# Attention rows turned by VectorE through DRAM instead of by TensorE: one change to a hybrid conformer and mLSTM kernel

## The chip, the cores and the metric

The kernel runs on one core of one Trainium2 chip. The metric is the device time of one execution in microseconds. A core has TensorE (PE, matmuls; PEld is its weight loads), VectorE (DVE), ScalarE (ACT), GpSimd (POOL) and SyncE (SP), each with an instruction queue of its own that is worked off in order. DMAs are issued here from SP's queue (nearly all loads) and from ACT's queue (stores to scratch in DRAM).

## The reference

Two post-norm layers run over 256 latent tokens and 256 context tokens of width 1024. Layer 0 mixes tokens with a Conformer convolution module, layer 1 with a bidirectional chunkwise mLSTM of 4 heads of width 512. Each mixer is followed by a squared-ReLU MLP, and all is modulated by adaLN vectors. The output is the latent stream. The part that matters here is the mLSTM's output, for each head:

```python
hsum = of[..., :MLSTM_INNER] * from_heads(h_f) + of[..., MLSTM_INNER:] * from_heads(h_b)
hh = hsum.reshape(bsz, s, MLSTM_HEADS, MLSTM_HEAD_DIM)
mu = jnp.mean(hh, axis=-1, keepdims=True)
var = jnp.mean(jnp.square(hh - mu), axis=-1, keepdims=True)
hn = ((hh - mu) * lax.rsqrt(var + LN_EPS)).reshape(bsz, s, MLSTM_INNER) * gn_g
y = (hn + skip * xc) * jax.nn.silu(z)
return y @ w_down
```

`h_f` and `h_b` are attention-like sums over chunks, weighted by `exp` of cumulated forget gates; `of` is a sigmoid gate computed from the latent tokens by a 2048 to 4096 product.

## The kernel before

All activations lie in SBUF; weights are streamed from DRAM in pieces of 128x2048 (1 MB) into one of three `raw` buffers. Every product is done in three matmuls of fp32r (`mm3`, `mm3t`): a value is split into a high part, cast by ACT (L151, tile `wh` for weights), and a low part, subtracted by DVE (L152, `wl`). Weight halves of 128x1024 have four buffers each (`NW = 4`).

The mLSTM of layer 1 first computes features and scores. Turned copies go to DRAM: `v_dr` (values, turned by DVE in 32x32 blocks at L1261 and stored by ACT's queue at L1265), `zs_dr` (the silu of z and skip * xc, feature by token), `r_dr` (the residual rows).

Then comes the stage of the change. It is a set of Python generators, zipped by a hand-written table:

```python
att = [['o0', 'G0 W0 T0 W1', 2], ['o1', 'A0 W2', 1.6], ['o2', 'A1 W3 D0', 2.1], ['o3', 'A2 V3', 2], ['D1 E3 D2', 'A3', 3], ['D3', '', 0]]
```

Each entry has a main chain, a side chain and how many side steps are taken per main step. `o` is `gate_o(h)`, 16 steps of twelve 128x512 matmuls (two directions d, four weight pieces q of two halves, psums `mm`, of which there are three; the bias row `bo` is loaded at L1491). `G` is `decay` (the forget gates' cumulated sums, ending in a store to `ng_dr`), `W` is `weights(h)` (the exponentials, DVE and ACT only, from rows of `ng_dr` loaded at L1510), `T` is `guards`, `V` is `values`, `A` is `attend(h)`, `D` is `down(h)`, `E` is `early`. The table gives the order in which work is written; a scheduler then orders each engine's queue by that priority and by when it expects operands, and puts in the waits.

`attend(h)` has 11 steps: the values are loaded and split; four groups of matmuls into psums `cv` are scaled and gated (L1624) and summed per token block into `hs[0]` and `hs[1]` (128 tokens x 512 features); statistics; the load of `zs_dr` into a `raw` buffer; ACT normalises `hs` (L1642). Then for each half `jp` TensorE turns four times two 128x128 blocks into PSUM (L1650, psums `ln`), DVE multiplies by `gn_g` and adds skip * xc (L1654), multiplies by silu(z) (L1656) and the result is split for `down(h)`. Tiles of this stage are in pool `og` (13 buffers): `y` is written over `og[h, 1, jp]`.

`decay` has five steps; the matmuls of the sums are at L1435 and L1436, after two bare steps. The residual rows `R` (1 MB) are loaded at L1573 in the second half of `gate_o(0)`; `down(0)` is their first reader. The 408 columns of vectors (`vecs`, biases, gains, convolution weights) come in two loads: the first 64 columns first of all (L117), the other 344 after the second step of the first product (L657).

At the start, `start0(f)` loads a 1 MB piece of adaLN weights (L145), a block of x (L623) and of the first product's weights (L625) for each of eight f; L344 multiplies the adaLN piece.

Of the kernel before, what the change touches and what calls it, by code (L numbers as in the profile page):

```python
# [8 lines left out]
F32 = mybir.dt.float32  # L9
# [3 lines left out]
ALU = mybir.AluOpType  # L13

P = 128
# [6 lines left out]
C = 256  # L22
H = 4
DH = E // H
# [32 lines left out]
_OFF = {}  # L57
# [14 lines left out]
def hybrid_kernel(ctx: ExitStack, tc: tile.TileContext, xT, vecs_d, wdw_d, ada0_w, ada_w, wg_d, pw1a, pw1, pw2, w1_0, w2_0,  # L72
                  w1_1, w2_1, up_x, up_z, wv, wo, bo_d, wk, wq, wqT, wdown, rows_d, out):
    nc = tc.nc
# [6 lines left out]
    dp = ctx.enter_context(tc.tile_pool(name="dp", bufs=1, space=bass.MemoryType.DRAM))  # L81
# [3 lines left out]
    def nm(s):  # L85
        uid[0] += 1
        return f"{s}_{uid[0]}"
# [13 lines left out]
    def psum(tag="mm"):  # L101
        return pp.tile([P, 512], F32, tag=tag, name=nm(tag), bufs={"mm": 3, "ln": 2, "fl": 1, "cv": 2}[tag])
# [10 lines left out]


    vecs = con.tile([P, NV], F32, name="vecs")
    NV0 = _OFF["ada_b1"][0]
    nc.sync.dma_start(vecs[:, :NV0], vecs_d[:, :NV0])  # L117

    def V(name, i=0, n=1):
        o = _OFF[name][0]  # L120
        return vecs[:, o + i:o + i + n]
# [5 lines left out]
    ident = con.tile([P, P], F32, name="ident")  # L127
# [484 lines left out]
    x, u = [], []  # L612
# [7 lines left out]
    def start0(f):  # L620
        t = X()
        raw = raw_load(ada0_w[f])
        nc.sync.dma_start(t, xT[f * P:(f + 1) * P, :])  # L623
        wr = F()
        nc.sync.dma_start(wr[:, :KO0 * P], pw1a[f])  # L625
        x.append(t)
        ps = psum("fl")[:, :2 * P]
        ada_mm(ps, [raw[:, kt * 2 * P:(kt + 1) * 2 * P] for kt in range(DT)])
        sb = F()[:, :2 * P]
        with tc.issue_after(folded):  # L630
            st[f] = wr, sb, nc.vector.tensor_copy(sb, ps).ins
# [22 lines left out]
    start1(0)  # L654
    idle(spare, 5)
    start0(1)
    nc.sync.dma_start(vecs[:, NV0:], vecs_d[:, NV0:])  # L657
    for f in range(DT):
        start2(f, (0,))
        if f + 1 < DT:  # L660
# [17 lines left out]
    fj, jj = ij[:, 0:L], ij[:, L:2 * L]  # L678
# [517 lines left out]
    for f in range(0, DT, 2):  # L1196
        t, tr = tmp("S"), psum("cv")
# [194 lines left out]
    def decay(_):  # L1392
        gT = tmp("L")
        nc.scalar.copy(gT, gps)
        yield
        gk = psum("ln")
        for b in range(4):
            nc.tensor.matmul(gk[:, b * 16:(b + 1) * 16], gT[:, b * P:(b + 1) * P], foldg, start=True, stop=True)
        gs = tmp("S")[:, 0:64].rearrange("p (b c) -> p b c", b=4)
        nc.vector.tensor_tensor(gs, gk[:, 0:64].rearrange("p (b c) -> p b c", b=4),  # L1400
                                VA("b_gate").rearrange("p (b c) -> p b c", b=4), op=ALU.add)
        gb_ = [tmp("L"), tmp("E"), tmp("E")]
        g8 = [gb_[i // 3][:, (i % 3) * 4 * NG:(i % 3 + 1) * 4 * NG].rearrange("p (b c) -> p b c", b=4) for i in range(8)]
        ig, fg, bsb, ex, up1, cor, lf, fa = g8
        nc.vector.memset(ig, 0.0)
        nc.vector.memset(fg, 0.0)
        for d in range(2):
            nc.vector.tensor_copy(ig[:, :, 32 * d:32 * d + 4], gs[:, :, 8 * d:8 * d + 4])
            nc.vector.tensor_copy(fg[:, :, 32 * d:32 * d + 4], gs[:, :, 8 * d + 4:8 * d + 8])


        nc.vector.scalar_tensor_tensor(fa, fg, -1.0, fg, op0=ALU.mult, op1=ALU.max)
        nc.scalar.activation(ex, fa, AF.Exp, scale=-1.0)
        nc.vector.tensor_scalar(up1, ex, 1.0, None, op0=ALU.add)
        nc.vector.scalar_tensor_tensor(cor, up1, -1.0, ex, op0=ALU.add, op1=ALU.subtract)
        nc.scalar.activation(lf, up1, AF.Ln)
        nc.vector.reciprocal(up1, up1)
        nc.vector.tensor_tensor(cor, cor, up1, op=ALU.mult)
        nc.vector.tensor_tensor(lf, cor, lf, op=ALU.subtract)
        nc.vector.tensor_scalar(fa, fg, 0.0, None, op0=ALU.min)  # L1420
        nc.vector.tensor_tensor(lf, lf, fa, op=ALU.add)

        nc.vector.memset(up1, 0.0)
        for d, (b0, b1, b2, b3) in ((0, (0, 1, 2, 3)), (1, (1, 0, 3, 2))):
            c = slice(32 * d, 32 if d == 0 else NG)
            nc.vector.tensor_copy(up1[:, b1, c], lf[:, b0, c])
            nc.vector.tensor_tensor(up1[:, b2, c], up1[:, b1, c], lf[:, b1, c], op=ALU.add)
            nc.vector.tensor_tensor(up1[:, b3, c], up1[:, b2, c], lf[:, b2, c], op=ALU.add)
        yield
        yield  # L1430
        bps = psum("ln")
        for d, cum in ((0, upper), (1, lower)):
            c = slice(32 * d, 32 if d == 0 else NG)
            reg = bps[:, 0:4 * NG].rearrange("p (b c) -> p b c", b=4)[:, :, c]
            nc.tensor.matmul(reg, cum, lf[:, :, c], start=True, stop=False)  # L1435
            nc.tensor.matmul(reg, ones, up1[:, :, c], start=False, stop=True)  # L1436
        nc.vector.tensor_copy(bsb, bps[:, 0:4 * NG].rearrange("p (b c) -> p b c", b=4))
        nc.vector.tensor_tensor(acol, ig, bsb, op=ALU.subtract)

        yield  # L1440
        aT = psum("ln")
        for b in range(4):
            nc.tensor.transpose(aT[:NG, b * P:(b + 1) * P], acol[:, b, :], ident)
        aR, mR = tmp("S"), tmp("S")
        nc.vector.tensor_copy(aR[:32, :], aT[:32, :])
        nc.vector.tensor_copy(aR[32:NG, LO], aT[32:NG, LO])
        nc.vector.tensor_copy(aR[32:NG, HI], aT[32:NG, T - 1:C - 1:-1])
        nc.vector.tensor_tensor_scan(mR[:NG, :], aR[:NG, :], aR[:NG, :], 0.0, op0=ALU.max, op1=ALU.max)
        nc.vector.tensor_scalar(negm[:32, :], mR[:32, HI], -1.0, None, op0=ALU.mult)
        nc.vector.tensor_scalar(negm[32:NG, :], mR[32:NG, T - 1:C - 1:-1], -1.0, None, op0=ALU.mult)  # L1450
        nc.scalar.dma_start(ng_dr, negm)
        bsbs.append(bsb)
        yield
# [104 lines left out]
    for i in range(2):  # L1558
        rx = raw_load(xl_dr[i].rearrange("p b c -> p (b c)"))
        for j in range(8):  # L1560
            t = XL(F32R)
            split(t[:, LO], t[:, HI], rx[:, j * C:(j + 1) * C])
            xls.append((t[:, LO], t[:, HI]))
    og, yy, rden, sums = {}, {}, {}, {}

    def gate_o(h):

        for d in range(2):
            bo = rows(BO().rearrange("p a b -> p (a b)"), bo_d[h:h + 1, d * DH:(d + 1) * DH])
            pss = [psum() for _ in range(2)]  # L1570
            if (h, d) == (0, 1):
                with tc.issue_after(loaded[0]):
                    nc.sync.dma_start(R, r_dr)  # L1573
            for q in range(4):
                ws = preo if (h, d, q) == (0, 0, 0) else None
                if ws is None:
                    raw = raw_load(wo[h, d, q])
                for i in range(2):
                    w = ws[i] if ws else split_w(raw[:, i * 1024:(i + 1) * 1024])
                    for t in range(2):  # L1580
                        for k in range(2):
                            kt = 4 * q + 2 * i + k
                            sl = slice(k * 512, (k + 1) * 512)
                            mm3t(pss[t], xls[kt][0][:, BLK[t]], xls[kt][1][:, BLK[t]], w[0][:, sl], w[1][:, sl],
                                 kt == 0, kt == ET - 1)
                        if q == 3 and i == 1:
                            og[h, d, t] = o_ = OG()
                            nc.vector.tensor_tensor(o_, pss[t], bo, op=ALU.add)  # L1588
                            nc.scalar.activation(o_, o_, AF.Sigmoid)
                    yield  # L1590

    vsp, zt = {}, []

    def values(h):
        rv = raw_load(v_dr[h].rearrange("p b c -> p (b c)"))
# [7 lines left out]
    def attend(h):  # L1603
# [7 lines left out]
        hs = []  # L1611
        for t in range(2):
            for d in range(2):
                ps = psum("cv")
                bl = [b for b in blocks[d] if rng[d, b][0] <= t * P < rng[d, b][1]]
                for i, b in enumerate(bl):
                    hi, lo = pw[h, d, b]
                    sl = slice(t * P - rng[d, b][0], t * P - rng[d, b][0] + P)
# [13 lines left out]
        if h == H - 1:  # L1632
            zz = zt
        else:
            rz = raw_load(zs_dr[h].rearrange("p b c -> p (b c)"))
            zz = [rz[:, i * T:(i + 1) * T] for i in range(4)]
# [5 lines left out]
            nc.scalar.activation(hs[t], hs[t], AF.Identity, scale=mv[:, t, 2:3], bias=mv[:, t, 3:4])  # L1642
        yield
        yy[h] = []
        for jp in range(2):
            tr = psum("ln")
            for jj in range(2):
                j = 2 * jp + jj
                for t in range(2):
                    nc.tensor.transpose(tr[:, jj * C + t * P:jj * C + (t + 1) * P], hs[t][:, j * P:(j + 1) * P], ident)  # L1650
            y = og[h, 1, jp]
            for jj in range(2):
                j, sl = 2 * jp + jj, slice(jj * C, (jj + 1) * C)
                nc.vector.scalar_tensor_tensor(y[:, sl], tr[:, sl], V("gn_g", 4 * h + j), zz[2 + jp][:, sl],  # L1654
                                               op0=ALU.mult, op1=ALU.add)
            nc.vector.tensor_tensor(y, y, zz[jp], op=ALU.mult)  # L1656
            hi, lo = OG(F32R), OG(F32R)
            split(hi, lo, y)
            yy[h] += [(hi[:, sl], lo[:, sl]) for sl in (LO, HI)]
            yield  # L1660
# [373 lines left out]
```

## Time and profile before

| | us |
|---|---|
| median of 3 runs | 1664.04 (1663.55 to 1665.42) |
| the profiled execution's own time | 1665.14 |
| its span, first to last instruction | 1663.4 |
| TensorE matmul busy | 1648.7 (99%) |
| VectorE busy | 1038.1 (62%) |
| ScalarE busy | 734.6 (44%) |
| granted TensorE clock | 0.999 |

A line of the profile names a source line, an engine, an operation, the tiles it writes and reads, a count, then busy time and mean duration. "a <- b" in the list of waits means that a sat idle until b was done: total, times, longest. The chain of waits is the sequence of work that ended last; a piece in it lasts until the next begins, so it gives the pace of pipelined matmuls where their own duration does not. Rows marked SPq or ACTq are a queue issuing DMAs, which is not counted as busy time. Times in windows are from the start of the span.

### The profile page before, as it was taken

How to read it: one execution, taken by the hardware profiler on the slowest of the kernel's cores; microseconds unless marked ns; L12 is line 12 of the kernel's file. 1: busy time of each engine (PE TensorE's matmuls, PEld its weight loads, DVE VectorE, ACT ScalarE, POOL GpSimd, SP SyncE). 2: the span in 40 equal slices, each digit the busy share in tenths (PEclk: the TensorE clock that was granted, in tenths of full speed). 3: DMA queues.
4: the chain of work that ended last, by engine and by line, in shares of the span. 5: the costliest groups of instructions: out<-in, count | busy, mean ns of one | idle time of the engine just before them, and what ended most of it. 6: DMA issues, size and time to landing. Idle time of an engine off the chain costs nothing.

```text
span 1663.4 us, 22731 instructions
## 1 busy us (share of the span) xinstructions
PE 1648.7 (99%) x8856; PEld 1357.6 (82%) x8856; DVE 1038.1 (62%) x1863; ACT 734.6 (44%) x1182; POOL 14.4 (1%) x64
## 2 busy tenths in 40 slices
PE   9999999999999999999999999999999999999998
PEld 6665898888888998877787899888877888878886
DVE  6554895666535765762354753553489876776677
ACT  4313573232324476652233533442477654555453
POOL 0000000000000000000000000000000000000001
PEclk9999999999999999999999999999999999999999
DMA  9555223534324065557774852554465555675552
GB/s 353 208 210 214 92 75 111 167 123 148 136 101 152 4 228 194 184 196 266 278 259 146 302 179 79 179 194 144 148 240 197 203 215 203 250 284 183 178 194 85
DMA packets 74331, 303.70 MB, mean 183 GB/s; under 512 B 7694, under 2 KB 23858, under 8 KB 44144
## 3 DMA queue, kind: packets, MB, share of 16 engines
q1 hardware_dynamic: 56368, 286.49, 49.1%
q10 hardware_dynamic: 17856, 15.77, 2.8%
q8 instruction: 69, 1.13, 0.3%
q14 instruction: 38, 0.31, 0.1%
HBM read 285.42 MB, written 16.81 MB: 182 GB/s over the span
## 4 chain that ended last, share of the span: by engine, by line
PE 95%; DVE 2%; DMA 1%; ACT 1%; issue 0%; SPq 0%; DVEq 0%; ACTq 0%
PE mm L182 18%; PE mm L185 17%; PE mm L186 17%; PE mm L197 7%; PE mm L198 4%; PE mm L215 3%; PE mm L213 3%; PE mm L214 3%; PE cv L213 2%; PE cv L215 2%; PE cv L214 2%; PE fl L344 1%; PE ln L182 1%; PE cv L860 1%; PE ln L214 1%; PE ln L185 1%
## 5 line engine op out<-in xcount | busy, mean ns | idle before, releaser
L152 DVE TENSOR_TENSOR wl<-raw,wh 128x1024 fp32r<-128x1024 f32 x344 | 418.7, 1221 | 245.5 <-ACT wh L151 233.4
L151 ACT CAST wh<-raw 128x1024 fp32r<-128x1024 f32 x344 | 358.6, 1051 | 469.3 <-PE mm L185 244.4
L185 PE MATMUL mm<-u,wh 128*128 128x512 f32 (+1 forms) x808 | 291.5, 361 | 0.2 <-DVE u L604 0.2
L182 PE MATMUL mm<-u,wh 128*128 128x512 f32 (+1 forms) x680 | 243.8, 359 | 0.0
L186 PE MATMUL mm<-u,wl 128*128 128x512 f32 (+1 forms) x680 | 241.3, 355 | 0.0
L185 PEld LDWEIGHTS mm<-u,wh 128*128 128x128 f32 x808 | 152.7, 189 | 23.2 <-issue 1.0
L182 PEld LDWEIGHTS mm<-u,wh 128*128 128x128 f32 x680 | 128.4, 189 | 24.4 <-issue 6.3
L186 PEld LDWEIGHTS mm<-u,wl 128*128 128x128 f32 x680 | 128.5, 189 | 17.8
L213 PE MATMUL mm<-wh,xl 128*128 128x512 f32 x256 | 101.0, 395 | 0.7 <-DVE og L1588 0.7
L182 PE MATMUL mm<-xm,wh 128*128 128x512 f32 x256 | 101.0, 394 | 0.0
L215 PE MATMUL mm<-wl,xl 128*128 128x512 f32 x256 | 100.0, 393 | 0.0
L214 PE MATMUL mm<-wh,xl 128*128 128x512 f32 x256 | 99.9, 390 | 0.0
L186 PE MATMUL mm<-xm,wl 128*128 128x512 f32 x256 | 99.7, 389 | 0.0
L182 PE MATMUL mm<-hid,wh 128*128 128x512 f32 (+1 forms) x256 | 93.3, 364 | 0.0
L186 PE MATMUL mm<-hid,wl 128*128 128x512 f32 (+1 forms) x256 | 92.8, 363 | 0.0
L185 PE MATMUL mm<-hid,wh 128*128 128x512 f32 (+1 forms) x256 | 92.8, 363 | 0.0
L197 PE MATMUL mm<-x,wh 128*128 128x512 f32 x232 | 81.1, 398 | 0.0
L185 PE MATMUL mm<-qq,wh 128*128 128x272 f32 x256 | 73.9, 289 | 0.0
L182 PE MATMUL mm<-qq,wh 128*128 128x272 f32 x256 | 73.5, 288 | 0.0
L186 PE MATMUL mm<-qq,wl 128*128 128x272 f32 x256 | 73.5, 288 | 0.0
L197 PE MATMUL mm<-u,wh 128*128 128x512 f32 x192 | 68.6, 399 | 0.0
L1099 DVE SCALAR_TENSOR_TENSOR x<-mm,ada,x 128x256 f32<-128x256 f32 x64 | 28.5, 479 | 63.4 <-PE mm L186 63.4
(537 smaller groups left out, 3249.4 us busy)
## 6 DMA issues: line engine op xcount, KB each, us to landing
raw<-w SPq DMA_DIRECT2D x64, 1024.0 KB, 4.9
raw<-wo SPq DMA_DIRECT2D x32, 1024.0 KB, 4.9
raw<-ada_w SPq DMA_DIRECT2D x22, 1024.0 KB, 7.0
ar<-ada_w SPq DMA_DIRECT2D x80, 256.0 KB, 3.9
raw<-wv SPq DMA_DIRECT2D x16, 1024.0 KB, 8.0
raw<-wqT SPq DMA_DIRECT2D x16, 1024.0 KB, 5.7
raw<-wq SPq DMA_DIRECT2D x16, 1024.0 KB, 5.8
raw<-wk SPq DMA_DIRECT2D x16, 1024.0 KB, 5.2
```

What stands on the lines that cost most here:

```text
L151: c = nc.scalar.copy(hi, src)
L152: lastsub[0] = nc.vector.tensor_tensor(lo, src, hi.bitcast(F32), op=ALU.subtract).ins
L182: a = nc.tensor.matmul(ps, wh, xh, start=start, stop=False)
L185: nc.tensor.matmul(ps, wh, xl, start=False, stop=False)
L186: lastmm[0] = nc.tensor.matmul(ps, wl, xh, start=False, stop=stop).ins
L197: todo = [lambda s_, e_: nc.tensor.matmul(ps, wh, r[0], start=s_, stop=e_), lambda s_, e_: nc.tensor.matmul(ps[:, :n], wl, r[0][:, :n], st ...
L198: lambda s_, e_: nc.tensor.matmul(ps[:, :n], wl, r[0][:, :n], start=s_, stop=e_)]
L213: nc.tensor.matmul(ps, xh, wh, start=start, stop=False)
L214: nc.tensor.matmul(ps, xl, wh, start=False, stop=False)
L215: nc.tensor.matmul(ps, xh, wl, start=False, stop=stop)
L344: a = mark_unit[0] = nc.tensor.matmul(ps[32 * j:32 * j + 32], cs[:, kt, 14 - 2 * v:46 - 2 * v], blocks[kt], start=first and kt < 4, stop=l ...
L1099: nc.vector.scalar_tensor_tensor(res[m][:, sl_], p_, g[:, m:m + 1], res[m][:, sl_], op0=ALU.mult, op1=ALU.add)
```

## The change

It has three parts. For heads 0 to 2 the normalised rows are turned by VectorE in 32x32 blocks into `og[h, 1, jp]`, stored by ACT's queue to a new scratch tensor `y_dr[h]` and loaded back by SP's queue over `hs[jp]`; the multiply-add with `gn_g` then reads SBUF and runs in pieces of 128 tokens. This adds four steps to `attend`. Head 3 stays as it was. `decay` gets one more bare step ahead of its sums, and the load of R moves from the second half of `gate_o(0)` to that of `gate_o(1)`. The vectors come in one load at the start.

```diff
     vecs = con.tile([P, NV], F32, name="vecs")
-    NV0 = _OFF["ada_b1"][0]
-    nc.sync.dma_start(vecs[:, :NV0], vecs_d[:, :NV0])
+    nc.sync.dma_start(vecs, vecs_d)
...
     start0(1)
-    nc.sync.dma_start(vecs[:, NV0:], vecs_d[:, NV0:])
...
         yield
         yield
+        yield
         bps = psum("ln")
...
-            if (h, d) == (0, 1):
+            if (h, d) == (1, 1):
                 with tc.issue_after(loaded[0]):
                     nc.sync.dma_start(R, r_dr)
...
     vsp, zt = {}, []
+    y_dr = [dp.tile([DH, C], F32, name=f"y_dr{h}") for h in range(H - 1)]
+
+    def turned_rows(h, hs):
+        for jp in range(2):
+            yt = og[h, 1, jp].rearrange("p (k t x) -> p k t x", k=8, t=2)
+            for t in range(2):
+                nc.vector.transpose(yt[:, :, t, :], hs[t][:, jp * C:(jp + 1) * C])
+            for r in range(4):
+                nc.scalar.dma_start(y_dr[h][jp * C:(jp + 1) * C, r * 64:(r + 1) * 64].rearrange("(k i) x -> i k x", i=32),
+                                    yt[32 * r:32 * r + 32].rearrange("i k t x -> i k (t x)"))
+            yield
+        yield
+        for jp in range(2):
+            nc.sync.dma_start(hs[jp].rearrange("p (j x) -> p j x", j=2), y_dr[h][jp * C:(jp + 1) * C, :].rearrange("(j p) x -> p j x", j=2))
+        yield
 
     def values(h):
         rv = raw_load(v_dr[h].rearrange("p b c -> p (b c)"))
...
             nc.scalar.activation(hs[t], hs[t], AF.Identity, scale=mv[:, t, 2:3], bias=mv[:, t, 3:4])
         yield
         yy[h] = []
+        if h < H - 1:
+            yield from turned_rows(h, hs)
         for jp in range(2):
-            tr = psum("ln")
-            for jj in range(2):
-                j = 2 * jp + jj
-                for t in range(2):
-                    nc.tensor.transpose(tr[:, jj * C + t * P:jj * C + (t + 1) * P], hs[t][:, j * P:(j + 1) * P], ident)
+            if h == H - 1:
+                tr = psum("ln")
+                for jj in range(2):
+                    j = 2 * jp + jj
+                    for t in range(2):
+                        nc.tensor.transpose(tr[:, jj * C + t * P:jj * C + (t + 1) * P], hs[t][:, j * P:(j + 1) * P], ident)
+            else:
+                tr = hs[jp]
             y = og[h, 1, jp]
             for jj in range(2):
                 j, sl = 2 * jp + jj, slice(jj * C, (jj + 1) * C)
-                nc.vector.scalar_tensor_tensor(y[:, sl], tr[:, sl], V("gn_g", 4 * h + j), zz[2 + jp][:, sl],
-                                               op0=ALU.mult, op1=ALU.add)
+
+                if h == H - 1:
+                    nc.vector.scalar_tensor_tensor(y[:, sl], tr[:, sl], V("gn_g", 4 * h + j), zz[2 + jp][:, sl],
+                                                   op0=ALU.mult, op1=ALU.add)
+                    continue
+                for t in range(2):
+                    y_, z_ = [a[:, jj * C + t * P:jj * C + (t + 1) * P].rearrange("p (r x) -> p r x", r=4)
+                              for a in (y, zz[2 + jp])]
+                    nc.vector.scalar_tensor_tensor(y_, tr[:, sl].rearrange("p (r t x) -> p t r x", r=4, t=2)[:, t],
+                                                   V("gn_g", 4 * h + j), z_, op0=ALU.mult, op1=ALU.add)
             nc.vector.tensor_tensor(y, y, zz[jp], op=ALU.mult)
             hi, lo = OG(F32R), OG(F32R)
             split(hi, lo, y)
```

## The prediction

> **What bounds the kernel now.** I read the head of the page and its chain first, then who TensorE waits for, then the windows around the change, and last single instructions.
>
> ```profile
> span 1663.4 us, 22731 instructions
> PE 1648.7 (99%) x8856; PEld 1357.6 (82%) x8856; DVE 1038.1 (62%) x1863; ACT 734.6 (44%) x1182; POOL 14.4 (1%) x64
> PE 95%; DVE 2%; DMA 1%; ACT 1%; issue 0%; SPq 0%; DVEq 0%; ACTq 0%
> PE ln L1435 <- DVE E L1421: 1.6, 1, 1.6
> PE fl L344 <- DMA raw<-ada_w: 1.4, 2, 1.2
> PE mm L213 <- DVE og L1588: 0.7, 1, 0.7
> ```
>
> TensorE (PE) is the bound: 95% of the chain that ended last is its matmuls. Its waits in the whole span are a handful; the three that touch this change are in decay (L1435), at the start (L344) and where head 1's gates take over head 0's PSUM banks (L1588). So work taken from PE shortens the kernel by what it occupied, as long as nobody makes PE wait instead. Who could is in the windows, whose columns are PE, PEld, DVE, ACT and POOL busy:
>
> ```profile
> 0.00:10.00 10.00, 7.70 (x60) 7.01 (x61) 3.15 (x19) 5.75 (x12) 2.52 (x13) 1.00 0.76 288
> 10.00:20.00 10.00, 9.76 (x80) 6.70 (x82) 7.70 (x29) 4.23 (x8) 0.00 (x0) 1.00 1.04 421
> 1220.00:1250.00 30.00, 29.33 (x128) 23.17 (x127) 25.95 (x56) 23.01 (x39) 0.00 (x0) 1.00 0.56 177
> 1250.00:1290.00 40.00, 39.99 (x188) 32.68 (x187) 36.74 (x74) 29.60 (x48) 0.00 (x0) 1.00 0.59 200
> 1290.00:1340.00 50.00, 50.00 (x226) 41.35 (x225) 41.29 (x73) 36.47 (x54) 0.00 (x0) 1.00 0.56 200
> 1340.00:1390.00 50.00, 50.00 (x224) 41.05 (x224) 31.91 (x39) 20.23 (x23) 0.00 (x0) 1.00 0.56 198
> ```
>
> Head 0 is attended in 1250 to 1290, head 1 in 1309 to 1340, head 2 around 1390 to 1415. PE has no gap in these, VectorE (DVE) is 92% busy in the first and 83% in the second. That is where the change puts new DVE and ACT work, so head 0 is the place of danger, and head 2 hardly.
>
> **Part 1, the transposes leave PE.** Per head eight 128x128 transposes (L1650) go, for heads 0 to 2: 24. What they occupy is read from the chain of waits, where a piece lasts until the next work starts:
>
> ```profile
> 1279.27 0.32 PE ln L1650 x2
> 1280.29 0.66 PE ln L1650 x6
> 1331.12 0.66 PE ln L1650 x6
> 1407.83 0.55 PE ln L1650 x3
> 1410.91 0.44 PE ln L1650 x4
> ```
>
> Head 0: 0.32 + 0.66 = 0.98 us for eight; the other pieces run at 0.11 to 0.18 us each, 0.9 to 1.4 for eight. I take 0.98 x 3 = 2.95 us less (bounds 2.7 to 3.6). The Trainium skill (VectorE: DVE Perf Modes, Rules for kernel authors) speaks against the move: it sends a 128x128 transpose to TensorE where PSUM is a good destination, and gives VectorE only 32x32 blocks within a bank. By that rule part 1 would be no gain at all and the sum 2.95 us higher; the rows above say what PE sheds, and the price elsewhere is worked out next.
>
> What comes in their place, per head: four DVE block transposes of 128x256, eight ACT-queue DMAs of 64 KB in 256-byte runs, two SP loads of 256 KB, eight 128x128 multiply-adds from SBUF instead of four 128x256 from PSUM.
>
> ```profile
> L1261 DVE STREAM_TRANSPOSE res<-vt x16: 702/706/714, 735.1 to 914.9; 128x512 f32<-128x512 f32 x16
> L1654 DVE SCALAR_TENSOR_TENSOR og<-ln,vecs,raw 128x256 f32<-128x256 f32 x4 | 1.7, 476 | 0.3 <-PE ln L1650 0.3
> L1525 DVE SCALAR_TENSOR_TENSOR S<-L,acol,mask 128x128 f32<-128x128 f32 x3 | 1.0, 344 | 0.0
> L1265 ACTq DMA_DIRECT2D v_dr<-res x16: 577/674/2011, 769.4 to 917.7; - x16
> 769.43 2.75 ACTq L1265 DMA_DIRECT2D v_dr<-res  x2
> v_dr<-res ACTq DMA_DIRECT2D x16, 256.0 KB, 6.3
> xc_dr<-E ACTq DMA_DIRECT2D x16, 256.0 KB, 3.6
> ```
>
> Transposes: half of 706 ns each, 4 x 0.35 = 1.4 us (up to 2.0 with a fixed part). Multiply-adds: 8 x 0.34 = 2.7 against 1.7 busy. Together about 2.4 us more DVE per head. ACT: no new arithmetic, but eight issues that sit in its in-order queue; the nearest row is v_dr's (turned blocks, same queue, twice the descriptors): 0.67 us, so 8 x 0.67 = 5.4 us per head, as low as half of that. Behind them on ACT wait the casts (L151) that feed PE's weights, and each first issue also waits for DVE's transposes.
>
> What hides this: weights are split ahead of their use. A half of a weight load occupies PE for twelve matmuls, 2.7 us, four halves are buffered, and ACT's casts mostly wait for PE to free one:
>
> ```profile
> ACT wh L151 <- PE mm L214: 9.1, 3, 4.4
> 1275.86 1.23 DVE L152 TENSOR_TENSOR wl<-raw,wh 128x1024 fp32r<-128x1024 f32 x1 [0.21 <-ACT wh L151]
> 1281.70 0.39 PE L213 MATMUL mm<-wh,xl 128*128 128x512 f32 x1
> 1291.46 1.22 DVE L152 TENSOR_TENSOR wl<-raw,wh 128x1024 fp32r<-128x1024 f32 x1
> 1293.55 0.39 PE L213 MATMUL mm<-wh,xl 128*128 128x512 f32 x1
> 1348.60 0.38 PE fl L213
> ```
>
> The first row is of 1310 to 1340: the longest wait is 4.4 us, so head 1 has about that as cover. For head 0 I counted halves, twelve matmuls each: the one whose low part is ready at 1275.86 + 1.23 = 1277.1 is used from 1281.70, a cover of 4.6 us; the one ready at 1291.46 + 1.22 = 1292.7 is used from 1293.55, a cover of 0.9. But the new steps also spread DVE's work: A0 gets four more side steps (11 to 15), 2.5 gate steps, so its multiply-adds and splits, and weights(2) behind them, move from 1280 to 1293 some 7 us on, to where DVE had gaps. The side list of gate_o(1) grows from 21 to 25 of 25.6 steps, of gate_o(2) from 25 to 29 of 33.6, of gate_o(3) from 12 to 16 of 32: all still fit. The turned rows are first needed in down(0), at 1348.6. I cost stalls at nothing, with 0 to 8.7 us as bounds (the ACT rival).
>
> **Part 2, decay's sums a half step later, and R's load moved.** PE waits 1.6 us at L1435 for DVE's L1421. One more side step is half a gate step, 1.4 us of matmuls whose weights are split already; they run in the hole. Most goes: 1.6 us. What is late next:
>
> ```profile
> 1204.49 0.43 SPq L1573 DMA_DIRECT2D res<-r_dr  x1
> 1207.03 2.00 ACT L151 CAST wh<-raw 128x1024 fp32r<-128x1024 f32 x2 [3.21 <-DMA raw<-wo]
> 1227.33 4.46 DMA L<-ng_dr
> 1248.63 0.61 DVE og L1588
> ```
>
> The chain runs from the weight load landing at 1207.0 through ACT and DVE's decay to the ng_dr rows (1227.3), DVE's weights(0) and the gate add at 1248.6, for which PE waits 0.7. If that DVE chain keeps its time, PE arrives 1.6 earlier and waits up to 2.3 there; the gain is then nil. Against that, R's load of 1 MB (issued 1204.49, in the middle of the loads ACT waits 3.2 us for) leaves this place for gate_o(1)'s second half; its queue there is SP's, behind the bias rows, with the loads for head 1's gates and V behind it, some 3 us at 400 GB/s, and its reader is down(0). The chain's start may come up to 1.5 us sooner. I take the 1.6 as gained, bounds 0.3 lost to 2.6 gained.
>
> **Part 3, the vectors in one load.**
>
> ```profile
> 2.67 7.83 DMA raw<-ada_w
> 4.39 0.44 SPq L657 DMA_DIRECT2D vecs<-vecs_d  x1
> 10.63 1.07 PE fl L344 x16
> vecs<-vecs_d SPq DMA_DIRECT2D x1, 172.0 KB, 7.9
> ```
>
> At the start the chain is the second weight load, issued at 2.67, landing at 10.5, then PE without a real gap. The 172 KB that were issued after it now go ahead of it: at 288 to 421 GB/s (windows above) 0.4 to 0.6 us later. I take 0.5 us lost; nothing after it waits on a load, so nothing gives it back. The issue saved at 4.39 us (0.44 us of SP) is before a load that PE does not wait for.
>
> **Sum:** -2.95 - 1.6 + 0.5 = -4.05 us. The profiled execution took 1665.14 (span 1663.4), so 1661.1 for it; the median of the runs shown, 1664.04, becomes 1660.0. About 0.2%, 3.3 us, is what a measurement of this kernel can tell from no change: faster means below 1660.7, slower above 1667.4.
>
> **Rivals.**
> *ACT's queue starves PE (slower).* Place: casts behind the two bursts of four issues in 1276 to 1293. A burst costs 2.7 us plus about 0.8 waiting for the transposes, two of them 7.0 us. Head 0 with 0.9 us of cover loses 6.1, head 1 with 4.4 loses 2.6, head 2 nothing: 8.7 - 4.05 = +4.65, 1668.7. It turns the sign once the stalls exceed 4.05 us. For it: DVE at 92%, the 2.75 us of two v_dr issues. Against it: the work moved out of 1280 to 1293, 10 us of ACT idle per 40, and smaller transfers. 0.24.
>
> *The load queue starves PE.* The hs loads sit in SP's queue until the writes have landed, 6.3 us by v_dr's row, with weight loads behind; and the zs rows keep one of three raw buffers some 7 us longer.
>
> ```profile
> 1257.54 0.32 SPq L145 DMA_DIRECT2D raw<-zs_dr  x1
> 1263.81 21.79 SPq L145 DMA_DIRECT2D raw<-wo  x5
> ```
>
> With two buffers left five loads went out in 21.8 us, 5.4 each, just the pace at which PE uses one. A block of 6.3 us against 4.6 us of cover costs 1.7 us for head 0; against 4.4 us it costs 1.9 for head 1: -4.05 + 3.6 = -0.45, 1663.6. The Trainium skill (VectorE: DVE Perf Modes, The three transpose paths) warns that a plain DMA doing a transpose by strides is 19 times slower than the crossbar's. The rows beside it, 6.3 against 3.6 us for 256 KB, say 1.75 times for turned blocks, which is the price used here. 0.12.
>
> *Decay's gain is handed back at L1588.* As in part 2: -2.95 + 0.5 = -2.45, 1661.6. For it: L1588 lies on the chain. 0.17.
>
> *R's move brings the whole first chain forward.* The 0.7 goes too, and some 1 us more of small waits: -5.8, 1658.2. 0.08.
>
> **How the numbers follow.** The forecast has 0.39, its own range 1658.8 to 1661.5 by the bounds of parts 1 to 3. Below 1660.7 lie the forecast and the last rival, 0.47; within 0.2% the two middle ones, 0.29; above, the ACT rival, 0.24. The range for 8 in 10 goes from just below the last rival, 1657.8, to the ACT rival, 1668.8; what it leaves out is worse stalls in head 0 and a larger gain.
>
> **What would show it.** L1650 with 8 transposes instead of 32 and no PE gap between 1250 and 1340: part 1 right. PE's wait at L1435 gone while that at L1588 stays near 0.7: part 2; a wait of 2 us or more at L1588 shows the hand-back. The second L344 group starting near 11.1 instead of 10.63: part 3. PE waiting for wh or wl (L151, L152) in gate_o(1), with ACT's DMA issues just ahead, shows the ACT rival; ACT waiting for raw behind an SP wait on y_dr, the load rival. The prediction is wrong if PE's removed time doesn't appear in the span, or if new PE waits exceed 4 us.

## The result and the profile after

The changed kernel takes 1683.0 us (median of four runs, 1680.63 to 1685.2) against 1664.73 for the kernel before beside it (1663.55 to 1665.72): ratio 1.0111, 95% interval 1.01 to 1.0123, 18 us slower. The prediction had 1660.0, with 1668.8 as the upper end of its range: wrong in sign and outside the range.

The profiled execution took 1684.34 us. The head of its page, and the list of whom TensorE waits for (total us, times, longest; line numbers from here on are those of the kernel after, one or two lower than before up to L1588):

```profile
span 1682.6 us, 22750 instructions
PE 1654.2 (98%) x8832; PEld 1361.8 (81%) x8832; DVE 1043.0 (62%) x1887; ACT 733.9 (44%) x1182; POOL 14.3 (1%) x64
PE mm L212 <- ACT wh L150: 10.3, 3, 6.3
PE mm L214 <- DVE wl L151: 3.3, 1, 3.3
PE ln L1434 <- DVE E L1419: 2.3, 1, 2.3
PE fl L343 <- DMA raw<-ada_w: 1.4, 2, 1.1
```

Two sums tell where the 19.2 us of span went. Span less PE busy was 1663.4 - 1648.7 = 14.7 and is 1682.6 - 1654.2 = 28.4: 13.7 us more of standing still, nearly all in the first two waits, which the kernel before did not have: TensorE short of split weights. And PE is busy 5.5 us longer with 24 transposes fewer: some of its matmuls ran slower. The windows (PE, PEld, DVE, ACT, POOL busy, clock, DMA share, GB/s) show where:

```profile
1220.00:1250.00 30.00, 29.92 (x127) 23.97 (x128) 22.15 (x45) 18.97 (x32) 0.00 (x0) 0.95 0.51 177
1290.00:1300.00 10.00, 4.04 (x9) 2.74 (x10) 6.62 (x14) 6.78 (x9) 0.00 (x0) 0.56 0.26 76
1350.00:1360.00 10.00, 7.48 (x26) 6.06 (x27) 9.20 (x17) 9.04 (x15) 0.00 (x0) 0.83 0.61 170
1430.00:1440.00 10.00, 6.68 (x23) 5.17 (x22) 7.33 (x16) 3.50 (x5) 0.00 (x0) 0.72 0.56 174
```

The last three rows hold one hole for each of the heads 0, 1 and 2, and in each the granted clock falls: to 0.56, 0.83 and 0.72. The first row is behind decay's wait of 2.3 us: there too the clock falls, to 0.95 where the kernel before had 1.00. The timelines (start, us, instruction, in brackets the idle time before it and who ended it) and a piece of the chain of waits show head 0's hole from end to end, and VectorE's waits at heads 1 and 2:

```profile
1280.71 1.42 DVE L1598 STREAM_TRANSPOSE og<-og 128x256 f32<-128x256 f32 x4
1284.26 1.22 DVE L151 TENSOR_TENSOR wl<-raw,wh 128x1024 fp32r<-128x1024 f32 x1
1292.41 1.14 DVE L1681 SCALAR_TENSOR_TENSOR og<-og,vecs,raw 128x128 f32<-128x128 f32 x4 [6.93 <-DMA og<-y_dr]
1349.00 1.14 DVE L1681 SCALAR_TENSOR_TENSOR og<-og,vecs,raw 128x128 f32<-128x128 f32 x4 [5.05 <-DMA y_dr<-og]
1432.63 1.14 DVE L1681 SCALAR_TENSOR_TENSOR og<-og,vecs,raw 128x128 f32<-128x128 f32 x4 [6.70 <-DMA og<-y_dr]
...
1281.51 7.13 ACTq L1600 DMA_DIRECT2D y_dr<-og  x8
1288.67 1.28 ACT L1588 ACT_TABLE_LOAD   x1 [6.77 <-DMA y_dr<-og]
1294.30 0.62 ACT L150 CAST og<-og 128x512 fp32r<-128x512 f32 x1 [3.19 <-DVE og L1683]
1294.83 2.93 ACT L150 CAST wh<-raw 128x1024 fp32r<-128x1024 f32 x3
...
1295.92 0.79 PE L212 MATMUL mm<-wh,xl 128*128 128x512 f32 x1 [6.31 <-ACT wh L150]
```

```profile
1283.16 0.23 PE mm L213
...
1288.33 4.09 DMA y_dr<-og
1292.44 2.40 DMA og<-y_dr
1294.84 1.04 ACT wh L150
1295.92 0.79 PE mm L212
1296.71 0.43 PE mm L213
```

VectorE turns the rows, splits one piece of weights, and then comes, in its fixed order, to the multiply-add, at 1285.5. The rows are back at 1292.4, 10.9 us after the first store was issued. Meanwhile ScalarE issues stores for 7.1 us and does nothing else; after one sigmoid it comes to its cast of the turned rows, which waits for VectorE, with the weight casts behind it. TensorE stands 6.3 us. At heads 1 and 2 VectorE's waits are 5.1 and 6.7 us. Two causes are in this one picture: ScalarE's burst of stores, and VectorE's wait in the middle of its queue. Then come matmuls at 0.43 us each; before the hole they ran at 0.23.

### The profile page after: what moved, and what is told of

It reads as the page before. It is cut to its first block, busy times and chain, and to the rows that moved or that the text cites. A ratio compares the mean times of both kernels' runs of the same rounds, so it can differ in the third digit from the quotient of the medians.

```text
span 1682.6 us, 22750 instructions
## 1 busy us (share of the span) xinstructions
PE 1654.2 (98%) x8832; PEld 1361.8 (81%) x8832; DVE 1043.0 (62%) x1887; ACT 733.9 (44%) x1182; POOL 14.3 (1%) x64
## 5 line engine op out<-in xcount | busy, mean ns | idle before, releaser
L212 PE MATMUL mm<-wh,xl 128*128 128x512 f32 x256 | 104.0, 407 | 10.7 <-ACT wh L150 10.3
L213 PE MATMUL mm<-wh,xl 128*128 128x512 f32 x256 | 102.9, 402 | 0.0
L212 PEld LDWEIGHTS mm<-wh,xl 128*128 128x128 f32 x256 | 50.2, 196 | 22.7 <-ACT wh L150 10.8
```

Of the source, the lines that this page charges most:

```text
L212: nc.tensor.matmul(ps, xh, wh, start=start, stop=False)
L213: nc.tensor.matmul(ps, xl, wh, start=False, stop=False)
```

## The experiments

All times are medians beside runs of the kernel before on the same chip (1664.0 to 1664.8). Line numbers in their rows are those of each kernel.

**Which part loses.** `e1_turn_only` undoes the change's parts 2 and 3, `e2_rest_only` has only these:

```diff
 # e1: the kernel after, with
-    nc.sync.dma_start(vecs, vecs_d)
+    nc.sync.dma_start(vecs[:, :NV0], vecs_d[:, :NV0])
     start0(1)
+    nc.sync.dma_start(vecs[:, NV0:], vecs_d[:, NV0:])
-        yield        # decay's extra step
-            if (h, d) == (1, 1):
+            if (h, d) == (0, 1):
 # e2: the kernel before with those three the other way round
```

> The changed kernel with its second and third part undone: only the turning by VectorE through DRAM remains. Queue-wait theory (VectorE reaches the multiply-add L1681 behind only one weight split, waits 5 to 7 us in order for the rows to come back from DRAM, ScalarE's casts wait behind it and TensorE runs dry): nearly all of the loss stays, 1678 to 1683 us, with waits of TensorE for wh or wl of 3 to 6 us at each of three heads. Rival that decay, R's load and the vectors do the harm: about 1662 to 1665 us.

> The kernel before with only the second and third part: decay's extra step, R's load moved, the vectors in one load. Queue-wait theory: these parts cost little, 1664 to 1667 us (TensorE's wait at decay's sums was 2.3 us in the changed kernel against 1.6 before, the start 0.05 us later). Rival that they do the harm: 1675 us or more. By the prediction's step for decay: 1663 us.

Measured: e1 1678.88 us, ratio 1.0085 [1.0066, 1.0104]; e2 1664.22, 0.9995 [0.9986, 1.0004]. The loss is in the turned rows; the other two parts alone can't be told from no change. Whether they cost something on top of the turn stays open: e1 is 14.6 us above before, the whole change 18.3, and the two intervals just overlap. Decay's wait, on which part 2 was costed, varies from run to run: 1.6 us in the profile of before, 2.3 in e1 that has the old decay, 2.3 after, and absent from e2's list.

**Without VectorE's wait.** `e3_no_wait` keeps transposes, stores and loads, but the multiply-add reads the unturned rows in place, so it waits for no load; the rows that come back are not used.

```diff
-                nc.sync.dma_start(hs[jp]..., y_dr[h]...)
+                nc.sync.dma_start(og[h, 1, jp]..., y_dr[h]...)
-            y = og[h, 1, jp]
+            y = og[h, 1, jp] if h == H - 1 else hs[jp]
...
-                    scalar_tensor_tensor(y_, tr[...][:, t], V("gn_g", 4 * h + j), z_, ...)
+                    scalar_tensor_tensor(y_, y_, V("gn_g", 4 * h + j), z_, ...)
```

> The changed kernel with every transpose, store and load kept, but the multiply-add works in place on the rows before they are turned, and the loads go over the stored tile, so nobody computes with what comes back: the result leaves out the turning. Queue-wait theory: VectorE no longer waits, TensorE's three long waits go, 1661 to 1667 us. Rival that ScalarE's eight store issues per head (7.1, 4.2 and 5.6 us in a row) starve the casts: still 1672 us or more, with ScalarE idle behind its stores while TensorE waits. Rival that the loads waiting in SyncE's queue starve the weights: also 1672 or more, with casts waiting for raw.

Measured: 1668.33, ratio 1.0023 [1.0011, 1.0035]: 4 us above before instead of 18, a little more than the 1661 to 1667 us expected. Its waits of TensorE, and one of ScalarE:

```profile
PE mm L212 <- DVE og L1587: 2.0, 1, 2.0
PE mm L214 <- DVE wl L151: 1.4, 4, 0.5
PE mm L212 <- ACT wh L150: 1.2, 1, 1.2
ACT wh L150 <- DMA y_dr<-og: 5.8, 1, 5.8
```

Without the wait the longest hole is 2.0 us. The profiled execution, 1665.66 us, was one of the faster ones, so this list may show less than the median lost. What is left is about 4 us, and the 2.95 us that the transposes should have brought. The bursts are still there, 3.9, 4.2 and 6.1 us; head 0's was 3.2 us shorter than in the kernel after, which may be part of the 14 us.

**The burst alone.** `e8_stores_only` is the kernel before, with TensorE's transposes, plus eight stores per head that nobody reads. `e12_half_stores` has four instead of eight, `e11_stores_pool` issues all eight by GpSimd's queue.

```diff
 # e8, after hs is normalised, heads 0 to 2
+        for jp in range(2):                    # e12: range(1)
+            for r in range(4):
+                nc.scalar.dma_start(y_dr[h][...],   # e11: nc.gpsimd
+                                    hs[jp][32 * r:32 * r + 32]...)
```

> The kernel before, with TensorE's transposes kept, plus the eight stores per head on ScalarE's queue that nobody reads: the price of the burst by itself. Queue-wait theory: 1664 to 1669 us, ScalarE 4 us late per head and its casts mostly in time. Rival of ScalarE's issues as the main cause: 1675 us or more.

> The kernel before plus the same eight unread stores per head, issued by GpSimd's queue instead of ScalarE's. If their price (+11.4 us from ScalarE's queue) is ScalarE standing still while it issues, with the casts of the weights behind it, this is within 1 us of before: 1664 to 1665.5. If it is the traffic of 64 KB stores in 256-byte runs taking bandwidth from the weight loads, whoever issues them, it stays 8 to 11 us above: 1672 to 1676.

> The kernel before plus four unread stores per head on ScalarE's queue instead of eight. In the run with eight, the first six were issued 0.5 us apart, then ScalarE stood about 4 us before the seventh at two of the three heads. If what costs is this stop, four stores have none: a burst of 4 x 0.5 = 2 us per head, no stop, and the time is 1664 to 1667, far less than half of the 11.4 us. If the price goes by the number of stores or bytes, it is half: 1669 to 1671, with a stop still inside the burst.

Measured: e8 1676.08, ratio 1.0068 [1.0054, 1.0083]; e11 1666.11, 1.0012 [1.0003, 1.0021]; e12 1664.06, 0.9997 [0.9988, 1.0007]. The same stores cost 11.4 us from ScalarE and 2.1 from GpSimd: what costs is ScalarE's time, not the traffic. e8 came out where the rival of ScalarE's issues had it, not where the queue-wait theory had it (1664 to 1669). The 2.1 exceed the 1 us expected, and e11's list has no new wait over 0.5 us that would explain them; its profiled execution took 1664.83, one of its fastest. Half the stores cost nothing rather than half. First the timeline of e8, then that of e12, ScalarE's bursts, with TensorE's longest hole in e8 as the last line of the first:

```profile
1279.44 7.28 ACTq L1647 DMA_DIRECT2D y_dr<-og  x8
1286.76 0.62 ACT L151 CAST og<-og 128x512 fp32r<-128x512 f32 x1 [6.64 <-DMA y_dr<-og]
1335.82 4.61 ACTq L1647 DMA_DIRECT2D y_dr<-og  x8
1415.21 7.00 ACTq L1647 DMA_DIRECT2D y_dr<-og  x8
1289.09 1.03 PE L213 MATMUL mm<-wh,xl 128*128 128x512 f32 x2 [3.38 <-ACT wh L151]
```

```profile
1277.90 1.83 ACTq L1647 DMA_DIRECT2D y_dr<-og  x4
1329.14 2.12 ACTq L1647 DMA_DIRECT2D y_dr<-og  x4
1406.99 1.84 ACTq L1647 DMA_DIRECT2D y_dr<-og  x4
```

Single starts in e8's first burst: 1279.4, 1279.8, 1280.3, 1280.8, 1281.3, 1281.9, then 1285.9 and 1286.3. Six go out half a microsecond apart, then ScalarE stops for 4 us. Head 2 has the same (the sixth at 1417.7, the seventh at 1421.4); head 1 has no such stop. In the kernel after, head 0 stops after the seventh (1284.4, 1288.3). Four stores never met it. That half costs nothing has two readings which this run doesn't part: no stop, and a burst of 2 us that fits into the cover of the weight casts. In the kernel after, the chain of waits puts the landing of a load of bias rows (bo, at 1288.31) just before the eighth store; that is inferred, and no run tests it. What ends the stop stays open.

**Only one of the two taken away.** `e4_pool_stores` is the kernel after with its stores on GpSimd's queue. `e5_apart` (the turn alone) cuts `attend` in two and puts the second half, from the loading of zs on, behind the next `weights`, so that more weight splits lie between.

```diff
 # e4
-                nc.scalar.dma_start(y_dr[h]...
+                nc.gpsimd.dma_start(y_dr[h]...
 # e5 (B: the second half of attend)
-    ... ['o1', 'A0 W2', 1.6], ['o2', 'A1 W3 D0', 2.1], ['o3', 'A2 V3', 1]
+    ... ['o1', 'A0 W2 B0', 1.7], ['o2', 'A1 W3 D0 B1', 2.1], ['o3', 'A2 V3 B2', 1.2]
```

> The changed kernel with the stores issued by GpSimd's queue instead of ScalarE's; in the built order VectorE's multiply-add now stands behind five weight splits instead of one. Queue-wait theory: the round trip is mostly covered, waits at L1681 under 3 us, 1662 to 1668 us. Rival of ScalarE's issues: the same gain, but then the gain would be there even where VectorE still waits. Rival of SyncE's queue: the loads wait as long or longer, still 1675 us or more.

> The turning alone (as in the run without the other parts), with attend cut in two: the second half (zs load, multiply-add, splits) follows weights of the next head in the side list. In the built order VectorE has 4, 6 and 1 weight splits between the transposes and the first multiply-add of heads 0, 1, 2, instead of 1 each. Queue-wait theory: heads 0 and 1 lose most of their stall, head 2 keeps its own of 3 to 5 us: 1665 to 1671 us. Rival of ScalarE's eight issues as the main cause: no change against the turning alone, 1677 to 1681.

Measured: e4 1674.82, ratio 1.0068 [1.0045, 1.009]; e5 1676.71, 1.0073 [1.0057, 1.0088]. Each gives back only part, and both miss what the queue-wait theory expected (at most 1668 and 1671); e5 is just below its rival's 1677. In e4 ScalarE is free, but VectorE still comes too early, now in head 1, whose rows were 14.1 us on their way from the first store to the multiply-add (list of waits and VectorE's timeline):

```profile
PE mm L212 <- DVE og L1587: 7.8, 2, 7.4
1345.62 1.14 DVE L1681 SCALAR_TENSOR_TENSOR og<-og,vecs,raw 128x128 f32<-128x128 f32 x4 [2.84 <-DMA og<-y_dr]
1348.78 1.28 DVE L1587 TENSOR_TENSOR og<-mm,bo 128x512 f32<-128x512 f32 x2
```

The gate adds that free TensorE's PSUM banks stand behind the multiply-adds: VectorE's wait of 2.84 us and the turned rows' own work ahead of the gate adds make a hole of 7.4. In e5 bursts of 5.6, 6.3 and 7.3 us remain; the multiply-adds of heads 0 and 1 no longer wait, head 2's still waits 6.7 us.

**Both taken away.** `e6_far` (the turn alone) puts the second half into the next head's gates and holds each multiply-add back until the last weight split written before it has issued; stores stay on ScalarE. `e7_far_pool` is e6 with the stores on GpSimd's queue.

```diff
+    ... ['o1', 'A0 W2', 1.6], ['o2', 'B0 A1 W3 D0', 2.1], ['o3', 'B1 A2 V3 P4 B2', 1.6]   # P4: four bare steps
+        last = lastsub[0]                # the last weight split
+                    with tc.issue_after(last):
                         nc.vector.scalar_tensor_tensor(y_, ...
```

> As before, further apart: the second half runs in the next gate_o's side list (head 2's at the end of gate_o(3)), and the multiply-add is ordered behind the last weight split written so far; 6, 10 and 6 splits lie between. Queue-wait theory: no wait at L1681, TensorE's long waits gone for all three heads; what is left are the store issues on ScalarE, as in the run that didn't wait: 1662 to 1668 us. Rival of ScalarE's issues as the main cause: 1675 us or more.

> The same with the stores issued by GpSimd: neither VectorE's wait nor ScalarE's burst is left. If these two are the whole loss, TensorE is relieved of 2.95 us and nothing replaces it: 1660 to 1663 us, faster than before. If SyncE's queue, held by the loads, or VectorE's 2 us more per head matter, 1665 us or more.

Measured: e6 1667.93, ratio 1.0018 [1.0009, 1.0026]; e7 1662.16, 0.9983 [0.9974, 0.9991]. In e6 VectorE waits for no turned row any more; bursts of 5.6, 6.2 and 3.9 us remain. Without them, in e7, the kernel is faster than before, although VectorE has all the work of the turn (1043.1 us busy, 1043.0 in the kernel after): that work by itself is not what cost. From 1250 to 1390 TensorE has no gap (windows of e7):

```profile
1250.00:1290.00 40.00, 40.00 (x185) 33.10 (x184) 35.23 (x72) 31.71 (x48) 4.83 (x8) 1.00 0.62 214
1290.00:1340.00 50.00, 50.00 (x222) 41.06 (x221) 41.14 (x75) 32.22 (x46) 2.03 (x4) 1.00 0.60 216
1340.00:1390.00 50.00, 50.00 (x224) 41.07 (x223) 37.54 (x56) 22.63 (x28) 2.57 (x5) 1.00 0.70 245
```

**Is it the transposes, and what do the other parts add?** `e10_later_only` has e7's cut and table, without its holding back of the multiply-adds, but TensorE keeps its transposes and nothing goes through DRAM; `e9_far_pool_all` is e7 with parts 2 and 3 of the change.

```diff
 # e10: e7 with
-            yield from turned_rows(h, hs)
-            if h == H - 1:        # transposes on TensorE for head 3 alone
+            if True:              # for all heads
```

> Control for the 2.5 us: the kernel before with the same cut of attend (the multiply-adds and all behind them in the next head's gates, the same table of side steps), but TensorE keeps the 24 transposes and nothing goes through DRAM. If the 2.5 us are TensorE's transposes gone, this is no faster than before: 1663 to 1666, ratio 0.999 to 1.001. If they come from the new order of the work, this too is near 1662, ratio 0.9983. If the late order costs something by itself, it is above 1666 and the transposes are worth more than 2.5 us.

> The late, GpSimd-stored turn (2.5 us below before) with the change's other two parts put back: decay's sums a half step later, R's load in head 1's gates, the vectors in one load. If these two parts are worth nothing, as their run alone said (0.9995), this lands within 2 us of the late turn without them: 1660 to 1664, ratio near 0.998. If the forecast's terms for them (-1.6 and +0.5) hold once nothing else stalls TensorE, it lands at 1661, ratio 0.9978. If R's load in head 1's gates delays the loads of turned rows, TensorE waits appear there and it is 1666 or more.

Measured: e10 1663.58, ratio 0.9998 [0.999, 1.0007]; e9 1660.56 (1659.37 to 1663.03), 0.9979 [0.9971, 0.9988]. The new order is worth nothing by itself, so the gain comes with the transposes. The two intervals overlap slightly at their ends; the traces agree, with TensorE 1649.4 us busy in e10 and 1646.7 in e7, 2.7 us less. e9 is the whole change with both causes removed, and beats both kernels: 3.5 us below before. It is 0.95 us further below before than e7 was, but the intervals overlap.

## Why the prediction was wrong, step by step

**Part 1, what TensorE sheds (2.95 us): borne out.** e7 is 2.5 us below before (interval 1.5 to 4.3), the control e10 0.45 below. The rule of the Trainium skill weighed there (VectorE: DVE Perf Modes, Rules for kernel authors: a 128x128 transpose belongs on TensorE) was read there as no gain at all; e7 shows a small one, once the way through DRAM makes nobody wait.

**"I cost stalls at nothing": the step that failed.** Its size was 13.7 us of standing still plus slower matmuls: 5.5 us more busy time although 2.95 should have gone, so about 8.4 us. It failed in three places.

First, the distance. The prediction let the added steps carry the multiply-adds "some 7 us on", away from 1280 to 1293. Steps in the table order the writing; the queue that came out had two gate adds and one weight split between transposes and multiply-add, and VectorE was there 4.0 us after the first store was issued, against a way through DRAM of 10.9. The prediction never summed that way: eight issues, the last write landing, the read back. So it had no VectorE wait in any case, not even in a rival. In e3, taking this wait away, and so that of ScalarE's cast with the weight casts queued behind it, took back 14 of the 18 us, less what head 0's shorter burst was worth.

Second, the burst. The ACT rival (0.24, 1668.7) had the right engine and place, and bursts of 5.4 to 7.0 us per head; 7.1, 4.2 and 5.6 were measured. It priced stalls at 8.7 us, with nothing for head 2, but head 2 had a hole of 3.3 us. Its cover for head 0, 0.9 us, was too small: in e8 a burst of 7.3 us left a hole of 3.4, so by these two rows about 3.9 us were covered, an estimate. The hint stood in its own row: v_dr's issues had a median of 0.67 us and a longest of 2.01, and two of them together took 2.75. The second of those two was the long one, which the median that I multiplied by eight can't show.

Third, what follows a stall. After 6.3 us without work the matmuls of head 0 took 0.43 us instead of 0.23, and after the 3.3 us of head 2 as well. No term of the sum had this. Of the 8.4 us, about 6.2 lie behind the three holes and 1.2 behind decay's wait (128x512 matmuls from start to start, less the same windows of before). The Trainium skill (TensorE: Matmul & The Clock Gate, What's actually happening) states that TensorE's clock is halved after an idle window of about 3.4 us and given back after as long a busy one. The halving agrees with 0.43 against 0.23. The times agree only in part: slow stretches in the kernel after, e4 and e8 lasted 3.4 to 5.7 us, and the clock fell after shorter waits too, decay's of 2.3 us in the kernel after and one of 2.2 us in e4 (at 1461.8, clock 0.58 from 1462 to 1466). The measurement decides here.

**The two causes don't add.** Both at once cost 14.6 us (e1). The burst without the wait cost some 3 to 4 (e3, e6), but 11.4 in the old order with the cast of the rows right behind it (e8); that the order makes this difference is argued, not tested. The wait without the burst cost 10.5 (e4). e3 and e4 contain the change's other two parts, the others don't. A cover of a few microseconds that is spent once, by whichever comes first, would give such figures.

**Part 2 (-1.6): not shown.** Parts 2 and 3 were to bring 1.1 us together; e2's interval reaches from 2.3 us gained to 0.7 lost, so they are neither seen nor excluded. The 1.6 us were one execution's value of a wait that was between none and 2.3 us in these profiles, whichever decay the kernel had. R's move brought nothing forward that is seen. Whether the gain is handed back at L1588, as that rival had it, can't be read from a gain that isn't seen; the sign given for it, a wait of 2 us or more there, is absent (0.4 us in the kernel after, none in e2).

**Part 3 (+0.5): not seen.** TensorE's wait for the adaLN pieces is 1.4 us in total after as before, 1.1 at the longest against 1.2. The second group of L343 starts at 10.69 us, against 10.63 before and 10.30 in e2; the sign given for part 3 was 11.1.

**The load-queue rival (0.12)** had the loads of the turned rows hold SP's queue. They did, 6.8 us for head 0. That was not tried by itself, but its sign is absent: from 1250 to 1310 ScalarE waits for no `raw` buffer in the kernel after. And e3, whose loads held the queue for 4.2 and 5.5 us (heads 0 and 2), has no hole longer than 2.0 us. In e9 the two loads of head 0 go out in 0.38 us each, at 1288.5 and 1297.5, and hold nothing.

**Slips in the working.** The table entry of `gate_o(3)` reads `['o3', 'A2 V3', 1]` in both kernels, not 2. Its side list thus grew from 12 to 16 of 16 steps, not of 32: full, where the prediction saw room. Two of the prediction's sums are off as well, without changing its outcome. The forecast's own range, 1658.8 to 1661.5, isn't what the bounds of its parts add up to, 1658.2 to 1662.2. VectorE's added work, 2.4 us per head, was 2.0: 1.4 for the four transposes and 2.3 instead of 1.7 for the multiply-adds.

## What to carry to other kernels

An engine relieved by a way through DRAM is relieved only if the reader's place in its own in-order queue lies further off than issue, write and read together: work that distance out from the order that is built, not from the order it is written in. Don't let an engine that feeds the bottleneck issue a burst of DMAs, and look at the longest issue of a row, not only its median. A stall of a few microseconds on a dense TensorE is paid again in the slow matmuls behind it: 8.4 us on 13.7 of standing still in the kernel after, 6.7 on 4.9 in e8. So a cover that is short by a little already turns the sign of a change worth 3 us.

## What was unexpected of the hardware

ScalarE's queue took six or seven 64 KB stores about 0.5 us apart and then stopped its engine, so that the next store started 2.1 to 4.2 us after the one before it, in 13 of the 18 bursts of eight in the kernel after, e1, e3, e5, e6 and e8; four stores (e12) went out in 1.8 to 2.1 us without a stop. GpSimd's queue took the same eight in 4.6 to 4.8 us, on an engine with nothing else to do:

```profile
L1647 POOL DMA_DIRECT2D y_dr<-og x24: 582/582/792, 1277.5 to 1409.4; - x24
L1647 ACTq DMA_DIRECT2D y_dr<-og x24: 309/468/1168, 1279.4 to 1421.7; - x24
```

The first row is of e11, the second of e8 (min, median, longest ns): per issue ScalarE is the faster. The Trainium skill (DMA: Bandwidth & Descriptors, Issuing engines are not separate DMA queues) says that issuing from several engines saves only the sequencer's issue time, usually small beside the transfer; here that time was what counted, 11.4 us against 2.1.

A 32x32-block transpose of 128x256 took 0.403 us where half of the 128x512 one gave 0.35: about 0.1 us is a fixed part, if both go by size.

```profile
L1598 DVE STREAM_TRANSPOSE og<-og x12: 401/403/439, 1280.7 to 1424.4; 128x256 f32<-128x256 f32 x12
```
